# RWKV inverse: sending the products of half of the chunks to the other head's partitions

## The chip, the core and the metric

The kernel runs on one core of a Trainium2 chip. A core has a matrix engine (TensorE, in the profile PE for matmuls and PEld for weight loads), VectorE (DVE), ScalarE (ACT), GpSimd (POOL) and DMA queues that SyncE (SP) issues. TensorE reads both operands from SBUF and writes into PSUM, which has eight banks of 2 KB on each of 128 partitions; DVE and ACT carry results from PSUM back to SBUF. The metric is the device time of one execution in microseconds, the median of several runs. All arithmetic here is fp32.

## The reference

The program is a two-layer backbone over 1024 latent tokens and 256 context tokens. The change touches one branch of the first layer, a bidirectional RWKV-7 scan with 8 heads of width 64:

```python
def step(S, inp):
    r_t, k_t, v_t, w_t, a_t, kk_t = inp
    Skk = jnp.einsum('dbhvk,dbhk->dbhv', S, kk_t)
    S = S * w_t[..., None, :] - Skk[..., :, None] * (kk_t * a_t)[..., None, :] + v_t[..., :, None] * k_t[..., None, :]
    return S, jnp.einsum('dbhvk,dbhk->dbhv', S, r_t)
```

The kernel doesn't step token by token. It cuts the tokens into 20 chunks of 64 and writes each chunk as matrix products. Within a chunk the corrections by earlier tokens form a unit triangular 64x64 system; its inverse is needed once for each chunk, head and direction.

## The kernel before

**Streams and units.** A column tile `ct` holds two heads, head 0 on partitions 0 to 63 and head 1 on 64 to 127. Two streams (`rwkv_stream`) each work through two column tiles, and `lockstep` advances them in turn. Each column tile has ten units: a unit (`rwkv_unit`) takes two chunks of each direction, so NJ = 4 pieces `j` (0 and 1 forward, 2 and 3 backward) for each of two heads. That makes 2 streams x 2 column tiles x 10 = 40 units. `pace` runs unit q+1 beside the chain of unit q (`rwkv_chain`), which carries the state from chunk to chunk through the PSUM tiles `ch`.

**What a unit does.** Decays are scanned and exponentiated (lines 692 to 706, DVE and ACT), operands AR, KB and RZ are built (711 to 717, POOL and DVE), and `pa` takes the products of AR and KB (729), which DVE masks into MN (732). MT is one minus the triangular part (744), `pk` holds transposes of KB (750) that ACT copies to KT (752).

**The inverse (762 to 781).** The transposed inverse TT starts from blocks of width 2 and doubles the width five times, b = 2, 4, 8, 16, 32. A doubling has three groups of products, called turns here: *px* multiplies MT by Tm (769) and DVE masks it into Xs (771); *pz* multiplies TT by Xs (775) and ACT copies it to the next Tm (777); *pt* multiplies Xs by TT (779) and ACT copies it back to TT (780). Before the first doubling a turn *px0* multiplies MT by the identity (764). The last doubling has no pz. So a unit has 1 + 4 x 3 + 2 = 15 turns. Each turn is 8 products of 64x64 by 64x64 (4 pieces, 2 heads). `halves` sends head 0's from partitions 0 to 63 to PSUM partitions 0 to 63 and head 1's from 64 to 127 to 64 to 127: of the four 64x64 quarters of the array, the two on the diagonal are used. In the trace a turn is 16 records, since an fp32 product is two records of PE and of PEld.

**PSUM.** Each stream has two banks under the tag `rec`. Every tile of that tag took one bank or less before, so there were two buffers, used in turn. A new tile in a buffer waits for the readers of the one before it.

**Order.** In this stage the Tile framework's scheduler orders each engine's instructions when the program is built; each engine then runs its own list strictly in that order as far as waits go, so an instruction that waits holds up what is behind it. Up to 1178 us the stage shares TensorE with the output projection of layer 0 (tiles `oa`); from there to about 1925 us it is alone.

Of the kernel before, what the change touches and what calls it, by code (L numbers as in the profile page):

```python
# [149 lines left out]
class K:  # L150
# [494 lines left out]
    def rwkv_unit(s, st, ct, gi):  # L645

        nc, rp = s.nc, s.rp
        X = s.RX[ct]
        L = 64 * NG
        NJ = 2 * NG  # L650
# [3 lines left out]
        H = [slice(0, 64), slice(64, 128)]  # L654
# [4 lines left out]
        def flat(t):  # L659
            return t.rearrange("p a b -> p (a b)")  # L660

        def rec(*sh):
            return s.psum(f"rec{st}", (128, NJ) + sh)

        r, k, kk = tl("ur", [64]), tl("uk", [64]), tl("ukk", [64])
        par = s.tn[st] % 2
        s.tn[st] += 1
# [1 line left out]
        TT, RZ, MT = s.tt[st, par], s.rz[st, par], s.mt[st]  # L669
        SV = X["sv", gi] = tl("SV", [2, 2, 64], 2)  # L670
# [52 lines left out]
        yield  # L723
        MN = tl("MN", [2, 2, 64], 2)
        mP = s.m("mP").rearrange("p (j a b) -> p j a b", a=2, b=64)
        pa = [rec(2, 64) for h in range(2)]
        for j in range(NJ):
            for h in range(2):
                s.mm(pa[h][:, j].rearrange("p a b -> p (a b)"), kb(j, h),
# [5 lines left out]
        def dj(t):  # L735
            return t.rearrange("p (d j) b -> p d j b", d=2)

        def bj(name):
            m_ = s.m(name).rearrange("p (d b) -> p d b", d=2)
            return m_.unsqueeze(2).to_broadcast([128, 2, NG, m_.shape[2]])  # L740
# [3 lines left out]
            nc.vector.scalar_tensor_tensor(MT[H[h]], MN[H[h], :, 0, h], -1.0,  # L744
                                           ident[H[h], H[h]].unsqueeze(1).to_broadcast([64, NJ, 64]), ALU.mult, ALU.add)
        KT = tl("KT", [2, 64], 2)
        pk = [rec(64) for h in range(2)]
        for j in range(NJ):
            for h in range(2):
                s.tr(pk[h][:, j], kb(j, h), ident[H[h], H[h]])  # L750
# [3 lines left out]
        nc.vector.tensor_mul(dj(TT), dj(MT), bj("m1"))  # L754
        yield

        def halves(fn):
            for j in range(NJ):
                for h in range(2):
                    fn(j, H[h])  # L760

        Tm = tl("Tm", [64], 2)
        px = rec(64)
        halves(lambda j, Q: s.mm(px[Q, j], MT[Q, j], s.m("id2")[Q]))
        nc.vector.tensor_mul(dj(Tm), dj(px), bj("l1"))
        yield
        for b in (2, 4, 8, 16, 32):
            px = rec(64)
            halves(lambda j, Q: s.mm(px[Q, j], MT[Q, j], Tm[Q, j]))
            Xs = tl("Xs", [64])  # L770
            nc.vector.tensor_mul(dj(Xs), dj(px), bj(f"l{b}"))  # L771
            yield
            if b < 32:
                pz = rec(64)
                halves(lambda j, Q: s.mm(pz[Q, j], TT[Q, j], Xs[Q, j]))
                Tm = tl("Tm", [64], 2)
                nc.scalar.copy(Tm, pz)
            pt = rec(64)
            halves(lambda j, Q: s.mm(pt[Q, j], Xs[Q, j], TT[Q, j]))
            nc.scalar.copy(TT, pt)  # L780
            yield
        X["u", gi] = {"E2": E2, "MN": MN, "KT": KT, "SV": SV, "TT": TT, "RZ": RZ}

    def rwkv_chain(s, st, ct, gi):
        nc, rp = s.nc, s.rp
        X = s.RX[ct]
        H = [slice(0, 64), slice(64, 128)]
        U = X["u", gi]
        SV, TT, MN, KT, E2, RZ = (U[k] for k in ("SV", "TT", "MN", "KT", "E2", "RZ"))
# [16 lines left out]
        for n in range(NG):  # L806
# [8 lines left out]
            pu = ch()  # L815
            for d, j in enumerate(js):
                for h in range(2):
                    s.mm(pu[H[h], d], TT[H[h], j], w[H[h], d])
            nc.vector.tensor_copy(both(SV, n)[H[0], :, 1, 0], pu[H[0]])
            nc.scalar.copy(both(SV, n)[H[1], :, 1, 1], pu[H[1]])  # L820
            yield
# [1226 lines left out]
```

## Time and profile before

| | us |
|---|---|
| median of 3 runs (3821.68 to 3825.0) | 3823.33 |
| the profiled execution's own time | 3834.97 |
| span of the profile | 3833.2 |
| PE busy in the span | 3442.4 (90%) |
| DVE, ACT, POOL busy | 2197.4, 1510.3, 1118.5 |
| the RWKV stage in the span, about | 966 to 1925 |

A row of the windows view gives a stretch of the span, its length, the busy time of each engine with the number of instructions, then the granted TensorE clock as a share of full speed, the share of the DMA engines and GB/s. A row of the timeline gives start, length, engine, line, operation, output and inputs, shapes and the number of instructions merged. A PE record's length includes the time until its result is in PSUM, so neighbouring records overlap and "busy" is not "issuing at its peak". A row of the view by tile gives minimum, median and maximum duration in ns, first and last start in us.

### The profile page before, as it was taken

What the parts mean: (1) busy time and instruction counts of PE and PEld (TensorE: products, weight loads), DVE (VectorE), ACT (ScalarE), POOL (GpSimd) and SP (SyncE); (2) the same over time, 40 slices, a digit from 0 to 9 for tenths busy, and PEclk for the clock granted to TensorE, in tenths of its full rate; (3) what the DMA queues carried; (4) which work ended last, traced back from release to release, by engine and by line L of the source; (5) the groups of instructions that cost most, each with busy time, mean ns of one, the idle gap of its engine ahead of it and who ended that gap; (6) DMA issues with size and microseconds to landing.
All of it is one profiled execution on the core that took longest, in us unless ns stands there. A gap on an engine that the chain in (4) does not pass through costs nothing. (4 is left out here: it accounts for less than half of the span.)

```text
span 3833.2 us, 74118 instructions
## 1 busy us (share of the span) xinstructions
PE 3442.4 (90%) x29178; PEld 2751.3 (72%) x29178; DVE 2197.4 (57%) x4053; ACT 1510.3 (39%) x3219; POOL 1118.5 (29%) x1071
## 2 busy tenths in 40 slices
PE   7999998887898998899869999999999788999978
PEld 3687876664577776688747798788888666676757
DVE  3576587773456666555556804533344387777645
ACT  3232333333434546444433322322222225666751
POOL 0112267552323221212102112212122255444330
PEclk9999998997798989789969999999999898999989
DMA  6526454436443222211132332554554451000023
GB/s 235 178 75 198 135 183 148 161 117 183 139 124 98 69 65 70 75 48 44 26 110 102 110 97 90 184 183 128 162 160 153 135 164 58 23 22 21 20 79 112
DMA packets 394277, 429.57 MB, mean 112 GB/s; under 512 B 81377, under 2 KB 317761, under 8 KB 391369
## 3 DMA queue, kind: packets, MB, share of 16 engines
q1 hardware_dynamic: 393928, 424.83, 35.4%
q8 instruction: 230, 3.77, 0.4%
q14 instruction: 119, 0.97, 0.1%
HBM read 306.62 MB, written 118.05 MB: 111 GB/s over the span
## 5 line engine op out<-in xcount | busy, mean ns | idle before, releaser
L211 PE MATMUL mm<-hh,wh 128*128 128x512 f32 (+1 forms) x1640 | 634.8, 387 | 0.0
L211 PE MATMUL mm<-hh,wl 128*128 128x512 f32 (+1 forms) x1640 | 609.9, 372 | 1.0 <-POOL wl L358 1.0
L211 PE MATMUL mm<-hl,wh 128*128 128x512 f32 (+1 forms) x1640 | 608.6, 371 | 0.0
L358 POOL TENSOR_TENSOR wl<-wr,wh 128x1024 fp32r<-128x1024 f32 x99 | 249.0, 2519 | 538.8 <-ACT wh L357 482.8
L211 PEld LDWEIGHTS mm<-hh,wh 128*128 128x128 f32 x1640 | 314.4, 192 | 66.7 <-issue 12.7
L211 PEld LDWEIGHTS mm<-hl,wh 128*128 128x128 f32 x1640 | 314.2, 192 | 61.6 <-issue 10.6
L211 PEld LDWEIGHTS mm<-hh,wl 128*128 128x128 f32 x1640 | 313.3, 191 | 60.1 <-issue 3.4
L1793 POOL TENSOR_SCALAR aP<-aP,adn,one 128x1280 f32<-128x1280 f32 x128 | 192.6, 1504 | 283.2 <-DVE adn L1792 159.6
L211 PE MATMUL mm<-wh,hh 128*128 128x256 f32 x736 | 218.3, 297 | 0.0
L1786 DVE TENSOR_REDUCE amx<-sc 128x1 f32<-128x1024 f32 x128 | 156.0, 1219 | 102.6 <-PE sc L211 102.5
L211 PE MATMUL mm<-wl,hh 128*128 128x256 f32 x736 | 209.7, 285 | 2.4 <-POOL wl L358 1.6
L211 PE MATMUL mm<-wh,hl 128*128 128x256 f32 x736 | 209.6, 285 | 0.0
L214 PE MATMUL tp<-mk,aP 128*128 128x128 f32 x1280 | 183.2, 280 | 4.1 <-ACT aPT L1801 4.1
L1801 ACT COPY aPT<-tp 128x512 f32<-128x512 f32 x256 | 145.8, 588 | 84.2 <-PE tp L214 82.2
L211 PE MATMUL pv<-aPT,aV 128*64 128x256 f32 x1280 | 169.6, 396 | 0.3 <-DVE aG L1817 0.3
L214 PEld LDWEIGHTS tp<-mk,aP 128*128 128x128 f32 x1280 | 144.4, 142 | 35.4 <-issue 21.5
L357 ACT CAST wh<-wr 128x1024 fp32r<-128x1024 f32 x99 | 103.2, 1045 | 152.5 <-PE mm L211 120.8
L211 PE MATMUL sc<-akT,aqs 128*128 128x512 f32 x512 | 154.0, 423 | 1.4 <-DVE aqs L1771 1.1
L1074 POOL TENSOR_SCALAR sel<-mk,mdfd,mdt 128x128 f32<-128x128 f32 x160 | 128.4, 819 | 76.3 <-DVE E L1098 45.8
L771 DVE TENSOR_TENSOR Xs<-rec,mk 128x256 f32<-128x256 f32 x200 | 84.3, 423 | 110.5 <-PE rec L211 107.1
L211 PE MATMUL oa<-wh,yh 128*128 128x512 f32 x288 | 127.9, 444 | 21.2 <-DVE o L1225 10.4
L211 PEld LDWEIGHTS mm<-wl,hh 128*128 128x128 f32 x736 | 141.8, 193 | 3.2 <-POOL wl L358 2.0
(422 smaller groups left out, 8039.7 us busy)
## 6 DMA issues: line engine op xcount, KB each, us to landing
wr<-in_wcd SPq DMA_DIRECT2D x60, 512.0 KB, 5.4
adaw<-in_ada SPq DMA_DIRECT2D x48, 512.0 KB, 5.4
R<-rowd SPq DMA_DIRECT2D x20, 1024.0 KB, 5.5
wr<-in_wab SPq DMA_DIRECT2D x38, 512.0 KB, 4.0
yr<-y SPq DMA_DIRECT2D x36, 512.0 KB, 4.0
xt<-xtok SPq DMA_DIRECT2D x20, 512.0 KB, 5.2
SV<-vtd SPq DMA_DIRECT2D x320, 32.0 KB, 2.2
lva<-lv SPq DMA_DIRECT2D x19, 514.0 KB, 4.6
```

Of the source, the lines that this page charges most:

```text
L211: return s.nc.tensor.matmul(out, lhsT, rhs, start=start, stop=stop)
L214: return s.nc.tensor.transpose(out, in_, ident)
L357: nc.scalar.copy(hi, raw)
L358: nc.gpsimd.tensor_sub(lo, raw, hi.bitcast(F32))
L771: nc.vector.tensor_mul(dj(Xs), dj(px), bj(f"l{b}"))
L1074: nc.gpsimd.tensor_scalar(sel[:, h], s.m("slt"), s.dfd[:, o:o + 1], dtb[:, h:h + 1], ALU.mult, ALU.add)
L1786: nc.vector.tensor_reduce(mx[:, 1:2], ps, AX.X, ALU.max)
L1793: nc.gpsimd.tensor_scalar(P, P, dn[:, 3:4], s.one, ALU.mult, ALU.mult)
L1801: copy(out, pp.rearrange("p (a b) q -> p a (b q)", a=out.shape[1]))
```

## The change

For half of the pieces the products go to the other head's PSUM partitions. `turn` takes the place of `halves`: it gets for both operands the place of each (j, h), a partition half and an index, and a set `to` of pieces whose result goes to the other half than their head's. It sorts the products by quarter of the array (input half, output half) and issues one of each quarter in turn: (0,0), (1,1), (0,1), (1,0). `side` names the pieces that are moved: from the pt of the first doubling on, every turn has two products in each of the four quarters, so 12 of the 15 turns; px0, px and pz of the first doubling stay on the diagonal. What was moved once is multiplied where it lies, and the last turn brings everything back to its own head's half; only the index of a piece within TT then differs, which `rwkv_chain` looks up in `iTT`.

A `rec` tile is now always two banks, `(128, 2, 512)`. The bank of a product is the half of the partitions that its inputs are on, so that two quarters that write the same partitions write different banks. With two banks to a stream there is one buffer instead of two. From the second doubling on pz and pt share one tile, pz in the first 128 columns of both banks, pt in the next 128, and the copy of pz to Tm is issued behind the turn pt. The masks and copies read 128 columns of each of two banks instead of 256 columns of one.

```diff
-        pa = [rec(2, 64) for h in range(2)]
+        pa = s.psum(f"rec{st}", (128, 2, 512))
+        pa = [pa[:, h].rearrange("p (j a b) -> p j a b", j=NJ, a=2) for h in range(2)]
...
-        pk = [rec(64) for h in range(2)]
+        pk = s.psum(f"rec{st}", (128, 2, 512))
+        pk = [pk[:, h, :64 * NJ].rearrange("p (j b) -> p j b", j=NJ) for h in range(2)]
...
-        def halves(fn):
+        def turn(A, ia, B, ib, to, out, slot=None):
+            place, quad = {}, {}
             for j in range(NJ):
                 for h in range(2):
-                    fn(j, H[h])
+                    (c0, i), (c1, k) = ia[j, h], ib[j, h]
...
+                    c = 1 - h if j in to else h
+                    place[j, h] = c, 2 * c0 + slot(j) if slot else j
...
+                    quad.setdefault((c0, c), []).append((i, k, place[j, h][1]))
...
+            for n in range(NJ):
+                for q in ((0, 0), (1, 1), (0, 1), (1, 0)):
+                    for i, k, o in quad.get(q, [])[n:n + 1]:
+                        s.mm(out[H[q[1]], o // 2, 64 * (o % 2):64 * (o % 2) + 64], A[H[q[0]], i],
+                             s.m("id2")[H[q[0]]] if B is None else B[H[q[0]], k])
+            return place
...
-        for b in (2, 4, 8, 16, 32):
-            px = rec(64)
-            halves(lambda j, Q: s.mm(px[Q, j], MT[Q, j], Tm[Q, j]))
+        side = ((), (1, 3), (0, 3), (1, 3), (0, 3), ())
+        for n, b in enumerate((2, 4, 8, 16, 32)):
+            px = pt_()
+            iX = turn(MT, own, Tm, iT, side[n], area(px, 0), (lambda j: j // 2) if n else None)
             Xs = tl("Xs", [64])
-            nc.vector.tensor_mul(dj(Xs), dj(px), bj(f"l{b}"))
+            mask(Xs, area(px, 0), f"l{b}", n > 0)
             yield
+            pz = pt_()
             if b < 32:
-                pz = rec(64)
-                halves(lambda j, Q: s.mm(pz[Q, j], TT[Q, j], Xs[Q, j]))
+                iT = turn(TT, iTT, Xs, iX, (), area(pz, 0), (lambda j: j // 2) if n else None)
+            if n == 0:
                 Tm = tl("Tm", [64], 2)
-                nc.scalar.copy(Tm, pz)
-            pt = rec(64)
-            halves(lambda j, Q: s.mm(pt[Q, j], Xs[Q, j], TT[Q, j]))
-            nc.scalar.copy(TT, pt)
+                nc.scalar.copy(Tm.rearrange("p (b s) l -> p b (s l)", b=2), area(pz, 0))
+                pt = pt_()
+            else:
+                pt = pz
+            iTT = turn(Xs, iX, TT, iTT, side[n + 1], area(pt, 1), (lambda j: j % 2) if 0 < n < 4 else (lambda j: j // 2))
+            if n and b < 32:
+                Tm = tl("Tm", [64], 2)
+                nc.scalar.copy(Tm.rearrange("p (b s) l -> p b (s l)", b=2), area(pz, 0))
+            nc.scalar.copy(TT.rearrange("p (b s) l -> p b (s l)", b=2), area(pt, 1))
             yield
...
-                    s.mm(pu[H[h], d], TT[H[h], j], w[H[h], d])
+                    s.mm(pu[H[h], d], TT[H[h], iTT[j, h][1]], w[H[h], d])
```

The scheduler's order changes with it. Three places are shown. In the rows, rec0 and MT0 belong to stream 0, rec1 and MT1 to stream 1; a number behind x counts products, and the bracket names the engines whose results an instruction waits for.

First, TensorE in the middle of a unit, where both streams are doubling: px of stream 1, then pz and pt of stream 0, then pz and pt of stream 1. Before:

```order
L211 MATMUL rec1_3357_18654<-Tm_3352_18621,MT1_6812 64x64 [waits DVE_49]
L211 MATMUL rec1_3357_18654<-Tm_3352_18621,MT1_6812 64x64 x7
L211 MATMUL rec0_3359_18665<-Xs_3356_18652,TT00_6791 64x64 [waits DVE_49,Activation_49]
L211 MATMUL rec0_3359_18665<-Xs_3356_18652,TT00_6791 64x64 x7
L211 MATMUL rec0_3361_18676<-TT00_6791,Xs_3356_18652 64x64 [waits PE_49]
L211 MATMUL rec0_3361_18676<-TT00_6791,Xs_3356_18652 64x64 x7
L211 MATMUL rec1_3363_18693<-Xs_3358_18663,TT11_6807 64x64 [waits DVE_49]
L211 MATMUL rec1_3363_18693<-Xs_3358_18663,TT11_6807 64x64 x7
L211 MATMUL rec1_3365_18704<-TT11_6807,Xs_3358_18663 64x64 [waits PE_49]
L211 MATMUL rec1_3365_18704<-TT11_6807,Xs_3358_18663 64x64 x7
```

The same place of the changed program, with the px of stream 0 that follows:

```order
L211 MATMUL rec1_3208_18574<-Tm_3203_18541,MT1_6812 64x64 [waits Activation_49]
L211 MATMUL rec1_3208_18574<-Tm_3203_18541,MT1_6812 64x64 x7
L211 MATMUL rec0_3210_18585<-Xs_3207_18572,TT00_6791 64x64 [waits DVE_49]
L211 MATMUL rec0_3210_18585<-Xs_3207_18572,TT00_6791 64x64 x7
L211 MATMUL rec0_3210_18585<-TT00_6791,Xs_3207_18572 64x64 x8
L211 MATMUL rec1_3213_18616<-Xs_3209_18583,TT11_6807 64x64 [waits DVE_49]
L211 MATMUL rec1_3213_18616<-Xs_3209_18583,TT11_6807 64x64 x7
L211 MATMUL rec1_3213_18616<-TT11_6807,Xs_3209_18583 64x64 x8
L211 MATMUL rec0_3217_18643<-Tm_3211_18602,MT0_6801 64x64 [waits PE_49,Activation_49]
L211 MATMUL rec0_3217_18643<-Tm_3211_18602,MT0_6801 64x64 x7
```

The order of the turns is the same; pt has no wait of its own any more, since it writes pz's tile.

Second, ScalarE's copies at that place, stream 0 and then stream 1. Before:

```order
L777 COPY Tm_3360_18674<-rec0_3359_18665 128x256 [waits PE_49]
L780 COPY TT00_6791<-rec0_3361_18676 128x256 [waits PE_49,Activation_49]
L777 COPY Tm_3364_18702<-rec1_3363_18693 128x256 [waits PE_49]
L780 COPY TT11_6807<-rec1_3365_18704 128x256 [waits PE_49]
L842 COPY y_2936_16167<-ch1_3366_18714 128x2x64 [waits PE_49]
```

And in the changed program:

```order
L816 COPY Tm_3211_18602<-rec0_3210_18585 128x256 [waits PE_49]
L817 COPY TT00_6791<-rec0_3210_18585 128x256
L816 COPY Tm_3214_18633<-rec1_3213_18616 128x256 [waits PE_49]
L817 COPY TT11_6807<-rec1_3213_18616 128x256 [waits Activation_49]
L817 COPY TT00_6791<-rec0_3221_18665 128x256 [waits PE_49,Activation_49]
```

Before, the copies to Tm and TT waited for a turn each; now both read one tile and both come behind pt, with Tm first.

Third, TensorE at the start of a unit of stream 1: the transposes pk (L214) and px0, which reads the identity in mk2. Before (pk of head 1, the chain's products and stream 0's turns between them):

```order
L214 MATMUL rec1_3346_18579<-mk_60,KB_3333_18505 128x64 [waits DVE_49]
L214 MATMUL rec1_3346_18579<-mk_60,KB_3333_18505 128x64 x3
L211 MATMUL ch0_3362_18686<-w_3351_18619,TT01_6796 64x64 x2
L211 MATMUL rec0_3347_18593<-Xs_3343_18573,TT00_6791 64x64 [waits DVE_49,Activation_49]
L211 MATMUL rec0_3347_18593<-Xs_3343_18573,TT00_6791 64x64 x7
L211 MATMUL rec0_3349_18604<-TT00_6791,Xs_3343_18573 64x64 [waits PE_49]
L211 MATMUL rec0_3349_18604<-TT00_6791,Xs_3343_18573 64x64 x7
L211 MATMUL rec1_3353_18622<-mk2_6776,MT1_6812 64x64 [waits DVE_49,Activation_49]
```

And in the changed program:

```order
L214 MATMUL rec1_3187_18420<-mk_60,KB_3176_18348 128x64 [waits DVE_49,PE_49]
L214 MATMUL rec1_3187_18420<-mk_60,KB_3176_18348 128x64 x7
L211 MATMUL rec0_3188_18434<-Xs_3185_18415,TT00_6791 64x64 [waits DVE_49]
L211 MATMUL rec0_3188_18434<-Xs_3185_18415,TT00_6791 64x64 x7
L211 MATMUL rec0_3188_18434<-TT00_6791,Xs_3185_18415 64x64 x8
L211 MATMUL rec1_3193_18462<-mk2_6776,MT1_6812 64x64 [waits DVE_49,PE_49,Activation_49]
```

The transposes of both heads now stand together behind the second mask of MN, and px0 waits for the copies of both heads to KT, since all share the one buffer.

More of the change, by code (lines that the diff above doesn't have):

```diff
@@ L660, in flat @@
             return t.rearrange("p a b -> p (a b)")
-        def rec(*sh):
-            return s.psum(f"rec{st}", (128, NJ) + sh)
         r, k, kk = tl("ur", [64]), tl("uk", [64]), tl("ukk", [64])
@@ L755, in rwkv_unit @@
         yield
-        def halves(fn):
+        def turn(A, ia, B, ib, to, out, slot=None):
+            place, quad = {}, {}
             for j in range(NJ):
                 for h in range(2):
-                    fn(j, H[h])
+                    (c0, i), (c1, k) = ia[j, h], ib[j, h]
+                    assert c0 == c1
+                    c = 1 - h if j in to else h
+                    place[j, h] = c, 2 * c0 + slot(j) if slot else j
+                    assert slot or c == c0
+                    quad.setdefault((c0, c), []).append((i, k, place[j, h][1]))
+            assert len(set(place.values())) == 2 * NJ
+            for n in range(NJ):
[4 more added lines that the diff above has]
+            return place
@@ new lines, in half, with mask, area, pt_ @@
+        def half(t):
+            return t.rearrange("p (b s) l -> p b s l", b=2)
+        def mask(t, out, name, banked):
+            m_ = s.m(name).rearrange("p (d b) -> p d b", d=2)
+            m_ = m_.unsqueeze(1).to_broadcast([128, 2, 2, 64]) if banked else m_.unsqueeze(2).to_broadcast([128, 2, 2, 64])
+            nc.vector.tensor_mul(half(t), out.rearrange("p b (s l) -> p b s l", s=2), m_)
+        def area(t, i):
+            return t[:, :, 128 * i:128 * i + 128]
+        def pt_():
+            return s.psum(f"rec{st}", (128, 2, 512))
@@ L762, in rwkv_unit @@
         Tm = tl("Tm", [64], 2)
-        px = rec(64)
-        halves(lambda j, Q: s.mm(px[Q, j], MT[Q, j], s.m("id2")[Q]))
-        nc.vector.tensor_mul(dj(Tm), dj(px), bj("l1"))
+        own = {(j, h): (h, j) for j in range(NJ) for h in range(2)}
+        px = pt_()
+        iT, iTT = turn(MT, own, None, own, (), area(px, 0)), own
+        mask(Tm, area(px, 0), "l1", False)
         yield
-        for b in (2, 4, 8, 16, 32):
-            px = rec(64)
-            halves(lambda j, Q: s.mm(px[Q, j], MT[Q, j], Tm[Q, j]))
+        side = ((), (1, 3), (0, 3), (1, 3), (0, 3), ())
@@ L770, in rwkv_unit @@
+        for n, b in enumerate((2, 4, 8, 16, 32)):
+            px = pt_()
+            iX = turn(MT, own, Tm, iT, side[n], area(px, 0), (lambda j: j // 2) if n else None)
             Xs = tl("Xs", [64])
-            nc.vector.tensor_mul(dj(Xs), dj(px), bj(f"l{b}"))
+            mask(Xs, area(px, 0), f"l{b}", n > 0)
             yield
+            pz = pt_()
             if b < 32:
-                pz = rec(64)
-                halves(lambda j, Q: s.mm(pz[Q, j], TT[Q, j], Xs[Q, j]))
+                iT = turn(TT, iTT, Xs, iX, (), area(pz, 0), (lambda j: j // 2) if n else None)
+            if n == 0:
@@ L781, in rwkv_unit @@
+            nc.scalar.copy(TT.rearrange("p (b s) l -> p b (s l)", b=2), area(pt, 1))
             yield
-        X["u", gi] = {"E2": E2, "MN": MN, "KT": KT, "SV": SV, "TT": TT, "RZ": RZ}
+        X["u", gi] = {"E2": E2, "MN": MN, "KT": KT, "SV": SV, "TT": (TT, iTT), "RZ": RZ}
     def rwkv_chain(s, st, ct, gi):
@@ L788, in rwkv_chain @@
         U = X["u", gi]
-        SV, TT, MN, KT, E2, RZ = (U[k] for k in ("SV", "TT", "MN", "KT", "E2", "RZ"))
+        SV, (TT, iTT), MN, KT, E2, RZ = (U[k] for k in ("SV", "TT", "MN", "KT", "E2", "RZ"))
         if gi == 0:
```

## The prediction

> **What bounds the kernel now.** I read the windows view first, because the change acts in one stage only. Its rows give the stretch, its length, PE, PEld, DVE, ACT and POOL busy, then clock, DMA share and GB/s; the rows of DVE alone are of the mask MN, two for each unit.
>
> ```profile
> 966.00:1178.00 212.00, 191.32 (x2083) 142.84 (x2084) 112.57 (x189) 83.89 (x189) 67.33 (x65) 0.86 0.43 130
> 1178.00:1925.00 747.00, 668.32 (x12960) 560.87 (x12960) 444.10 (x1013) 367.12 (x1025) 162.61 (x203) 0.89 0.22 59
> 1500.00:1600.00 100.00, 76.44 (x1079) 59.39 (x1080) 61.42 (x126) 52.98 (x122) 26.23 (x32) 0.76 0.29 85
> 1632.00:1895.00 263.00, 245.43 (x5150) 211.89 (x5147) 147.54 (x364) 117.85 (x364) 51.79 (x66) 0.94 0.15 39
> 1178.00:1925.00 747.00, 45.24 (x70) 0.89 0.22 59
> 1632.00:1895.00 263.00, 18.01 (x28) 0.94 0.15 39
> ```
>
> From 1178 us on the stage stands alone: 747 us with 35 of the 40 units. PE is busy 93% of the calm stretch 1632 to 1895, DVE 56%, ACT 45%. There 14 units, so 7 periods of one unit of each stream, take 263 us: **37.6 us a period**. "Busy" counts drains, so I ask the view of groups for that stretch what the remaining idle time waits for, and the timeline whether TensorE issues without a pause.
>
> ```profile
> L211 PE MATMUL rec<-AR,KB 64*128 64x128 f32 x224 | 22.3, 308 | 14.3 <-POOL AR L713 13.9 <-DVE KB L715 0.3
> ```
>
> ```profile
> 1719.89 1.11 PE L211 MATMUL rec<-Tm,MT 64*64 64x64 f32 x16
> ...
> 1723.41 1.15 PE L211 MATMUL rec<-Tm,MT 64*64 64x64 f32 x32
> 1724.48 0.33 PE L211 MATMUL ch<-SV,mk 128*64 128x64 f32 x2
> 1724.74 0.68 PE L211 MATMUL rec<-Xs,TT 64*64 64x64 f32 x16
> 1725.26 0.63 PE L211 MATMUL rec<-TT,Xs 64*64 64x64 f32 x16
> ...
> 1726.43 0.68 PE L211 MATMUL rec<-Xs,TT 64*64 64x64 f32 x16
> 1726.94 0.63 PE L211 MATMUL rec<-TT,Xs 64*64 64x64 f32 x16
> 1727.51 0.45 PE L211 MATMUL ch<-SV,MN 128*64 128x64 f32 x8
> 1727.89 1.15 PE L211 MATMUL rec<-Tm,MT 64*64 64x64 f32 x32
> ```
>
> Of the 17.6 us that PE is idle (263 less 245.43), 13.9 are one wait, AR for POOL at the start of a unit. From 1723.41 to 1727.89, a *joint step* (both streams do one doubling), one group follows the other without a hole: px of both (x32), pz and pt of one stream, products of the chain, pz and pt of the other, chain. So in joint steps TensorE's issue is what ends last, and a turn that issues faster shortens the step.
>
> **What a turn costs, and what four quarters make of it.** The second turn in an x32 row adds 1.15 - 0.68 = 0.47 us, and it is 8 pairs of records (one of each diagonal quarter), so a pair takes 0.059 us. With four quarters used, four records share such a slot: 4 slots instead of 8, **0.235 us less for each of 12 turns**. For 40 units that is 480 x 0.235 = 113 us, or 127 at the mean clock of 0.89: the most that can be gained.
>
> Four at once is not in the trace. Two halves of it are:
>
> ```profile
> 1729.84 0.27 PE L211 MATMUL ch<-SV,MN 128*64 128x64 f32 x1
> 1729.85 0.27 PE L211 MATMUL ch<-SV,RZ 128*64 128x64 f32 x1
> 1729.94 0.22 PE L211 MATMUL ch<-SV,MN 128*64 128x64 f32 x1
> 1729.95 0.22 PE L211 MATMUL ch<-SV,RZ 128*64 128x64 f32 x1
> ...
> 1737.07 1.16 PE L211 MATMUL rec<-AR,KB 64*128 64x128 f32 x14
> ```
>
> Chain products on the two column halves, which share all rows, start 0.01 us apart, and the second product's first record starts ahead of the first product's second: a free tile doesn't wait for a busy one. AR,KB uses two row halves, which share all columns and write two banks: 14 records of 128 columns would take at least 14 x 0.118 = 1.65 us one by one (twice the slot each), and took 1.16, so they run in pairs. The bounds are therefore 0 and 0.235 us a turn; I take 0.235, as each sharing that four quarters need stands in one of these rows.
>
> The Trainium skill, TensorE: Matmul & The Clock Gate, Part 3: Packing small matmuls, says that a weight load overlaps matmuls in flight only where the row group differs. Quarters (0,0) and (0,1) share a row group, so by that rule a turn would stay at 0.47, which is the slower rival below; the rows of 1729.84 disagree, since both products load all rows.
>
> **The terms, for one period.** Durations of the other engines come from the view by tile, a lone step (only one stream left doubling) from the timeline.
>
> ```profile
> L771 DVE TENSOR_TENSOR Xs<-rec,mk x200: 405/425/426, 983.7 to 1910.4; 128x256 f32<-128x256 f32 x100
> L777 ACT COPY Tm<-rec x160: 354/372/387, 985.8 to 1909.2; 128x256 f32<-128x256 f32 x160
> L732 DVE TENSOR_TENSOR MN<-rec,mk x80: 654/682/694, 969.6 to 1889.9; 128x512 f32<-128x512 f32 x80
> ```
>
> ```profile
> 1731.66 0.63 PE L211 MATMUL rec<-Tm,MT 64*64 64x64 f32 x16
> ...
> 1733.00 0.68 PE L211 MATMUL rec<-Xs,TT 64*64 64x64 f32 x16
> 1733.51 0.63 PE L211 MATMUL rec<-TT,Xs 64*64 64x64 f32 x16
> ...
> 1734.57 0.68 PE L211 MATMUL rec<-Tm,MT 64*64 64x64 f32 x16
> ```
>
> ```profile
> 1733.72 0.37 ACT L777 COPY Tm<-rec 128x256 f32<-128x256 f32 x1 [1.27 <-PE rec L211]
> 1734.25 0.37 ACT L780 COPY TT<-rec 128x256 f32<-128x256 f32 x1
> ```
>
> *The new chain of one stream.* A turn's result is read 0.05 us after its end (pz ends 1733.68, Tm starts 1733.72). With one buffer, px waits for the copy to TT as well, and Tm is copied behind pt. One doubling is then px 0.45 (0.68 less 0.235), mask 0.425, pz and pt 0.23 + 0.45, Tm 0.37, TT 0.37, and four handovers of 0.05: **2.5 us**.
>
> *Joint steps.* Six turns shrink by 1.41: 4.48 becomes 3.07. That stays above one stream's 2.5, above two masks (0.85) and above four copies (1.49) with the chain's few. For restarts of 0.05 (0.68 against 0.63) and worse packing I give back 0.2: -1.2 each. From 1719.89, when the second stream joins, to 1731.66, when the first is done, there are three in a period: **-3.6**.
>
> *Lone steps.* 1731.66 to 1734.57 is 2.91 us. The chain gives 2.5, with chain products in the gaps 2.6: -0.3, twice a period: **-0.6**. Here the waits for pt and the copy to TT, 0.23 + 0.37, eat most of what the turns save.
>
> *First steps of the earlier stream.* Between these two px, of one stream, the other sets up its unit:
>
> ```profile
> 1711.33 1.12 PE L211 MATMUL rec<-Tm,MT 64*64 64x64 f32 x16
> ...
> 1718.29 1.06 PE L211 MATMUL rec<-Tm,MT 64*64 64x64 f32 x16
> ```
>
> A doubling takes 7 us there, at half clock (a turn of 1.06 instead of 0.63) and behind setup. Four turns with four quarters save 0.94 to 1.9; most goes into the same wait for POOL, so between 0 and 1.9 I take **-0.5**.
>
> *Setup.* All transposes now wait for the second MN mask, 0.68 later than the first, and px0 for the copies of both heads to KT: 0 to about 1.1 us. Behind pk stand the other stream's turns, which cover a part: **+0.5**. In the first doubling pt waits for Tm's copy and the next px for TT's: 0 to 0.9 (turn 0.45, copy 0.37, handovers); this falls into the stalled stretch, so **+0.3**.
>
> *Masks and copies on two banks.* From L771 and L732 256 more elements cost 0.257, so the fixed part is 0.17: a second piece could cost nothing or up to 0.17. The element count is the same, so I take 0; the other end adds 0.5 to each doubling's chain. Less than nothing is excluded, as no element is saved.
>
> *Clock.* TensorE will pause more. 24 turns a period lose 5.6 of 35.1 us busy, so busy falls from 93% to 29.4 of 33.7, 87%; rows at 90% and 76% had clocks of 0.86 and 0.76, though with long DMA gaps. **+0.5**, bounds 0 and 3.
>
> Sum: -3.6 - 0.6 - 0.5 + 0.5 + 0.3 + 0.5 = **-3.4 us a period**. 35 units are 17.5 periods: -60. In the five units ahead of 1178 TensorE is shared with the output projection and DMA is at 0.43; half of it, 2.5 x 1.7: -4. Together **-64 us**: 3835 of the profiled execution becomes 3771, and from the median of 3823.3, which lies 0.3% lower, **3759**.
>
> **Rivals.** *Only two quarters run at a time* (the change doesn't do what it says). Turns stay at 0.47, the waits remain. Joint steps don't care: TensorE's 4.48 covers the chain, which is then 3.2 us (px 0.68, mask 0.425, pz and pt 0.47 + 0.68, copies 0.74, handovers 0.2). Two lone steps cost +0.3 each, setup and first doubling +0.8: +1.4 a period, +24 us, **3847, slower**. It decides if a turn gets less than some 0.06 us shorter, since 24 turns must pay 1.4. For it: no row shows three tiles at work. Against: the overtaking rows above.
>
> *The clock follows the busy share.* At 0.84 instead of 0.94 a period of 33.7, of which I take 80% as TensorE-bound, gets 3.2 longer: net -0.7, -12 us, **3811**. For: the row of 1500 to 1600. Against: the low clock there goes with long holes, while joint steps stay dense.
>
> *Evacuation takes over.* If each mask and copy costs 0.17 more, each of five doublings takes 0.5 longer, 2.5 a period: -0.9 is left, -16 us, **3807**. For: ACT already follows each turn. Against: ACT is busy 45% only. The Trainium skill, TensorEngine Tiling (Array Packing), PSUM Bottleneck, says that after such a speedup the copies out of PSUM may become the bottleneck; the 2.5 us chain, nearly half of it copies and a mask, leans that way, and the joint 3.07 does not.
>
> **How the numbers follow.** Forecast 62% at 3759, its own range 3705 to 3795 (-6.5 to -1.5 a period); two quarters 14%; clock 11%; evacuation 13%. 3705 to 3830 leaves out most of the slower case and the deepest gains, about two tenths. A measurement tells some 0.2%, 8 us, from no change. Slower: the first rival and tails of the last two, 17%; within: 8%; faster: 75%.
>
> **What would show it.** A four-quarter turn of 16 records should read about 0.40 to 0.45 us instead of 0.63 to 0.68, in an unbroken pair of turns 0.23 apart; if it reads 0.63, the first rival holds. px of both streams should recur every 3.1 us in joint steps and every 2.6 in lone ones; the row of MN should give 14 units in some 239 us. A clock below 0.88 in the calm stretch speaks for the second rival, DVE masks near 0.6 us or ACT copies near 0.54 for the third. The forecast falls if joint steps are rarer than three a period, or if the new order puts a waiting AR,KB ahead of turns that were ready.

## The result, and the profile after

| | us | ratio to before (95%) |
|---|---|---|
| forecast | 3759, range 3705 to 3830 | |
| before, median of 4 runs beside the changed kernel | 3822.98 | |
| changed, median of 4 runs (3788.40 to 3804.39) | 3795.82 | 0.9929 (0.9907 to 0.9951) |
| profiled execution, before and changed | 3834.97 and 3797.94 | |

The kernel is 27 us faster, 0.7%, where 64 us were forecast. The direction and the range held, the size did not: less than half came. The execution traced before lay 12 us above its median, the one of the changed kernel 2, so the traces differ by 37 us, some 10 more than the medians.

First the rows that answer to those of before. The windows view of the changed kernel (columns as before; the second piece is the row of the mask MN, DVE busy only):

```profile
966.00:1178.00 212.00, 181.74 (x2074) 131.73 (x2076) 117.01 (x192) 81.04 (x187) 70.39 (x67) 0.86 0.44 131
1178.00:1894.00 716.00, 601.67 (x12972) 473.79 (x12970) 446.45 (x1013) 354.20 (x1029) 158.63 (x203) 0.83 0.23 63
1500.00:1600.00 100.00, 71.32 (x1060) 51.84 (x1060) 50.77 (x102) 43.48 (x107) 21.09 (x27) 0.62 0.25 72
1624.00:1858.00 234.00, 18.04 (x28) 0.95 0.18 45
```

The stage ends 31 us earlier, and the calm stretch did better than forecast: the same 28 masks, 14 units, take 234 us instead of 263; the forecast was 239. What is new is the clock of the whole stage, 0.83 instead of 0.89, and 0.62 instead of 0.76 in the stretch around 1550.

The view by tile (minimum, median, maximum in ns) and the timeline of TensorE in joint steps of the changed kernel:

```profile
L783 DVE TENSOR_TENSOR Xs<-rec,mk x200: 361/425/426, 980.8 to 1881.2; 128x256 f32<-128x256 f32 x100
L816 ACT COPY Tm<-rec x120: 353/373/393, 990.0 to 1877.8; 128x256 f32<-128x256 f32 x120
L730 DVE TENSOR_TENSOR MN<-rec,mk x80: 627/681/693, 971.6 to 1853.0; 128x512 f32<-128x512 f32 x80
```

```profile
1706.82 0.46 PE L211 MATMUL rec<-Tm,MT 64*64 64x64 f32 x16 [0.22 <-ACT TT L817]
1707.10 0.41 PE L211 MATMUL rec<-Xs,TT 64*64 64x64 f32 x16
1707.33 0.41 PE L211 MATMUL rec<-TT,Xs 64*64 64x64 f32 x16
1708.32 0.46 PE L211 MATMUL rec<-Xs,TT 64*64 64x64 f32 x16 [0.57 <-DVE Xs L783]
...
1709.78 0.46 PE L211 MATMUL rec<-Tm,MT 64*64 64x64 f32 x16
```

A turn takes 0.41 to 0.46 us instead of 0.63 to 0.68, and of an unbroken pair the second starts 0.23 behind the first (1707.10 and 1707.33): four quarters do run at once. Masks and copies on two banks cost what they did (0.425, 0.373 and 0.681 against 0.425, 0.372 and 0.682). But where TensorE issued without a pause before, two rows now have a wait in brackets: for the copy to TT, and for the mask Xs.

Equal places of the program are better than equal times. These rows go from the first MN mask of unit 6 of the stage's order to that of unit 20 (beside the features of the second column tiles), to that of unit 26 (the change of column tiles), to that of unit 38, counting both streams' units as they come, from 0: 14, 6 and 12 units. Before, changed, and the first experiment, which has the changed kernel's buffer but only two quarters:

```profile
1187.30:1473.80 286.50, 262.51 (x5156) 220.44 (x5156) 179.67 (x412) 147.72 (x411) 66.86 (x84) 0.90 0.25 68
1473.80:1637.20 163.40, 135.48 (x2288) 108.72 (x2286) 101.05 (x210) 85.95 (x217) 37.94 (x47) 0.82 0.26 74
1637.20:1862.90 225.70, 211.03 (x4370) 181.91 (x4372) 125.61 (x314) 101.47 (x313) 46.49 (x60) 0.93 0.17 42
```

```profile
1187.60:1464.20 276.60, 243.04 (x5176) 192.34 (x5178) 179.39 (x412) 142.12 (x412) 65.03 (x84) 0.83 0.26 71
1464.20:1629.40 165.20, 124.56 (x2268) 93.69 (x2268) 100.72 (x210) 83.53 (x216) 37.33 (x47) 0.74 0.25 72
1629.40:1828.60 199.20, 179.78 (x4395) 144.42 (x4398) 127.71 (x314) 95.75 (x315) 45.08 (x60) 0.94 0.19 49
```

```profile
1191.30:1493.80 302.50, 274.84 (x5174) 226.79 (x5176) 180.94 (x412) 143.68 (x413) 65.64 (x84) 0.87 0.24 65
1493.80:1665.30 171.50, 138.28 (x2280) 110.49 (x2280) 99.43 (x211) 82.50 (x214) 37.48 (x47) 0.78 0.25 69
1665.30:1884.10 218.80, 206.16 (x4384) 174.25 (x4381) 127.51 (x313) 96.49 (x315) 45.18 (x60) 0.97 0.17 44
```

Beside the features the changed kernel gained 9.9 us in 7 periods, at the column change it lost 1.8 in 3, in the calm stretch it gained 26.5 in 6. At 3.4 a period these would have been 24, 10 and 20. So the calm stretch, from which the forecast was read, kept its promise, and the other two stretches did not. The diagonal kernel shows that such a stretch can't be read alone: in the calm one it is faster than the kernel before (218.8 us against 225.7), and slower in both others.

### The profile page after: what moved, and what is told of

Same layout as the page of the kernel before. It is cut to its first block, busy times and chain, and to the rows that moved or that the text cites. A ratio compares the mean times of both kernels' runs of the same rounds, so it can differ in the third digit from the quotient of the medians.

```text
span 3796.1 us, 74040 instructions
## 1 busy us (share of the span) xinstructions
PE 3366.2 (89%) x29178; PEld 2650.6 (70%) x29178; DVE 2208.6 (58%) x4053; ACT 1493.0 (39%) x3219; POOL 1116.6 (29%) x1071
## 5 line engine op out<-in xcount | busy, mean ns | idle before, releaser
L214 PE MATMUL tp<-mk,aP 128*128 128x128 f32 x1280 | 181.0, 278 | 5.0 <-ACT aPT L1838 5.0
L214 PEld LDWEIGHTS tp<-mk,aP 128*128 128x128 f32 x1280 | 142.5, 141 | 35.9 <-issue 20.4
```

Source lines behind the costliest of these rows:

```text
L214: return s.nc.tensor.transpose(out, in_, ident)
```

## The experiments

Ratios are to the kernel before on the same chip (3829 to 3837 us there), with 95% intervals.

### Quarters and buffer apart

The changed kernel with `side` empty keeps to the diagonal, with the buffer, the waits and the late copy to Tm of the change:

```diff
-        side = ((), (1, 3), (0, 3), (1, 3), (0, 3), ())
+        side = ((),) * 6
```

(places within a tile then follow the piece number in every turn, and masks are laid out for that.)

> The changed kernel, but no piece is sent to the other half: every turn keeps to the two quarters on the diagonal; the one buffer of two banks, the tile shared by pz and pt, and the late copy to Tm stay. It prices the buffer and the new waits alone. By the working on record this is the first rival: +1.4 us a period, 3847 us, and the calm stretch at some 39 us a period instead of 37.6. If the waits are what ate the missing 37 us of the forecast, they must cost more than that: the four quarters are worth some 60 to 110 us as in the calm stretch (4.4 us a period and more), so this kernel would read 3860 to 3900. If the missing gain lies elsewhere (the column change, the clock), it reads 3830 to 3850.

Measured: 3861.3, **1.0087** (1.0069 to 1.0104). The buffer and its waits cost 33 us, and the four quarters give back 1.0087 - 0.9929 = 1.58%, 60 us. That lies at the lower edge of the 3860 to 3900 that were expected if the waits ate the gain. By the prediction's own working the first rival put the waits at 24 us, and the quarters at 64 + 24 = 88. So of the 37 us that are missing some 9 lie with the waits and some 28 with the quarters, each with an error of some 10.

Next, the features of the second column tile begin earlier, in both kernels:

```diff
-            if gi == 4 and ct != cts[-1]:
+            if gi == 1 and ct != cts[-1]:
```

> The changed kernel, with the features of the second column tile begun beside unit 1 instead of unit 4. Theory A (the column change): the changed kernel finished its units of the first column tile 10 us earlier, but then waited for the features of the second, whose first unit began at 1543 us as before; with the features begun earlier that wait goes, and the time falls by 8 to 20 us to some 3776 to 3788. Theory B (the clock takes the gain back beside the features): the features cost the same wherever they lie, so the time stays within 6 us of 3796.

> The kernel before, with the same earlier features: the control of the run above. Theory A: before the change the inverse was slow enough to let the features finish nearly in time, so little is to be had: 3815 to 3825. If it gains as much as the changed kernel does (8 to 20 us), the column change cost both kernels alike and isn't where the forecast lost its gain.

Measured: changed 3786.14, **0.9886** (0.9866 to 0.9906); before 3803.7, **0.9929** (0.9915 to 0.9944). Theory A falls: the kernel before gains even more, so the column change cost both alike. As a pair they differ by 17.6 us.

Then the same pair with no features of the second column tiles at all: the ten groups are left out, and the second tiles read the data of the first.

```diff
-                side.append(s.alone(s.rwkv_prep(st, cts[cts.index(ct) + 1])))
+                s.RX[cts[1]] = {}
+                for x in (s.kk_d, s.vt_d, s.bv_d):
+                    x[cts[1]] = x[cts[0]]
```

> The kernel before, without the features of the second column tiles: their ten groups of projections are left out, and the second column tiles read the key directions, values and bonus terms of the first (that part of the computation is wrong). So no unit runs beside features, and the column change waits for none. It is one half of a pair with the next run. Units beside features should then cost about as much as those after the column change, 37 us a period: from the first MN mask of unit 12 to that of unit 52 some 365 us instead of 450, so a total of some 3740 to 3775.

> The changed kernel, with the same part left out. Theory E (the gain is lost beside the features: there TensorE's holes and the half clock take back what the four quarters save, and the column change waits for the features, not for the inverse): without features every period gains what the periods after the column change gained, 4.4 us, so the pair differs by 55 to 80 us, or 1.5 to 2.1%. Rival (the four quarters save less than thought everywhere, and the large gain after the column change was chance of one execution's clock): the pair differs by 18 to 40 us, as the two whole kernels do.

Measured: before 3738.53, **0.9773** (0.9750 to 0.9795); changed 3715.52, **0.9716** (0.9692 to 0.9740). (Where these expectations say unit 12 or 52, they count masks, two to a unit: units 6 and 26 here.) Theory E falls too: the pair differs by 23 us, not 55 to 80. From the first mask of unit 26 to that of unit 38 the kernel before now takes 209.4 us, where it took 225.7, though nothing of that stretch was edited, and the changed one 198.6, as it did:

```profile
1559.50:1768.90 209.40, 193.81 (x4363) 168.74 (x4360) 125.16 (x314) 100.45 (x312) 48.56 (x61) 0.94 0.18 46
```

```profile
1550.20:1748.80 198.60, 174.89 (x4358) 146.17 (x4358) 125.07 (x314) 96.38 (x312) 49.26 (x60) 0.90 0.19 49
```

With the features begun early the kernel before takes 209.7 us there as well:

```profile
1632.60:1842.30 209.70, 194.11 (x4390) 169.06 (x4392) 125.65 (x313) 100.78 (x313) 47.52 (x60) 0.95 0.18 45
```

TensorE's list is indeed another in that stretch. In the kernel before, the earlier stream's px stands ahead of the later stream's transposes, which come in two pieces; without second features (second fence), and with the features early too, the transposes stand together ahead of that px:

```profile
1750.72 0.68 PE L211 MATMUL rec<-Tm,MT 64*64 64x64 f32 x16
1751.79 0.46 PE L214 MATMUL rec<-mk,KB 64*128 64x64 f32 x4
1752.92 0.46 PE L214 MATMUL rec<-mk,KB 64*128 64x64 f32 x4
```

```profile
1630.86 0.70 PE L214 MATMUL rec<-mk,KB 64*128 64x64 f32 x8
...
1631.49 1.11 PE L211 MATMUL rec<-Tm,MT 64*64 64x64 f32 x16
```

So the 37 us a period on which the forecast stands belong to one order of the list; in two others the same kernel runs at 35. Of the 26.5 us gained there some 16 go with the order; in the two other orders the change gains 11 us (209.4 to 198.6) and 15 (209.7 to 195.0).

The diagonal kernel in these two surroundings:

> The changed kernel on the diagonal alone (all turns in two quarters, but one buffer and its waits), without the features of the second column tiles (that part of the computation is wrong). It stands between the pair that differed by 23 us, 3738.5 and 3715.5. Theory F (two parts with opposite signs in any order: the waits cost some 30 us, the quarters give back 50 to 60): 3762 to 3780. Rival (in the regular order without features the waits hide, and the quarters are worth little): 3738 to 3752.

> The changed kernel on the diagonal alone, with the features of the second column tile begun beside unit 1. It stands between the kernel before with that edit, 3803.7, and the changed kernel with it, 3786.1. Theory F: 3826 to 3850. Rival: 3800 to 3818.

Measured: 3775.93, **0.9844** (0.9829 to 0.9859), and 3841.91, **1.0015** (1.0000 to 1.0030). With them the split is there three times, each number a difference of ratios times 3830 (by the intervals, some 10 us either way):

| | buffer and waits | four quarters | net |
|---|---|---|---|
| as it is | +33 | -60 | -27 |
| features early | +33 | -49 | -16 |
| no second features | +27 | -49 | -22 |

That the change nets some 20 us, out of +30 and -50 to -60, is thus shown in three orders of the list. The traces, one execution each, say the same of the stage alone: from the first MN to the last product of a chain the buffer costs 26, 34 and 38 us, and the quarters give back 59, 53 and 53.

### Where in a period

Without second features several steps repeat from period to period to 0.01 us, so places can be compared. The table has means over the last four periods of the calm stretch, from the starts of the first records of the turns (px0, px) and of MN; "later" is the stream that joins last. Us:

| stretch of a period | before | changed | before, no 2nd features | diagonal, no 2nd | changed, no 2nd |
|---|---|---|---|---|---|
| three joint steps | 11.34 | 9.35 | 12.29 | 12.58 | 9.99 |
| last px but one of the later to MN of the earlier | 6.40 | 5.04 | 5.90 | 6.29 | 5.58 |
| of it, to the last px (a lone step) | 2.91 | 3.08 | 2.49 | 3.67 | 3.40 |
| MN to the first doubling | 4.80 | 5.84 | 5.83 | 5.82 | 5.82 |
| first doubling of the earlier to that of the later | 14.42 | 12.43 | 11.08 | 12.76 | 12.64 |
| period | 36.97 | 32.65 | 35.09 | 37.46 | 34.02 |

The last three columns tell buffer from quarters by place. Of the 2.4 us a period that the buffer costs there, 1.7 lie between the two first doublings; of the 3.4 that the quarters give back, 2.6 lie in the joint steps.

The lone step, timeline of the pair without second features, before and then changed:

```profile
1611.51 0.68 PE L211 MATMUL rec<-Tm,MT 64*64 64x64 f32 x16
...
1612.84 0.68 PE L211 MATMUL rec<-Xs,TT 64*64 64x64 f32 x16
...
1613.36 0.63 PE L211 MATMUL rec<-TT,Xs 64*64 64x64 f32 x16
1613.57 0.37 ACT L777 COPY Tm<-rec 128x256 f32<-128x256 f32 x1 [1.49 <-PE rec L211]
1614.00 0.68 PE L211 MATMUL rec<-Tm,MT 64*64 64x64 f32 x16
1614.09 0.37 ACT L780 COPY TT<-rec 128x256 f32<-128x256 f32 x1
```

```profile
1597.56 0.46 PE L211 MATMUL rec<-Tm,MT 64*64 64x64 f32 x16
...
1599.15 0.46 PE L211 MATMUL rec<-Xs,TT 64*64 64x64 f32 x16
1599.43 0.41 PE L211 MATMUL rec<-TT,Xs 64*64 64x64 f32 x16
...
1599.91 0.37 ACT L816 COPY Tm<-rec 128x256 f32<-128x256 f32 x1 [1.07 <-PE rec L211]
...
1600.18 0.38 ACT L817 COPY TT<-rec 128x256 f32<-128x256 f32 x1
...
1600.62 0.48 PE L211 MATMUL rec<-AR,KB 64*128 64x128 f32 x2
...
1601.03 0.46 PE L211 MATMUL rec<-Tm,MT 64*64 64x64 f32 x16
```

From pz to the next px it took 1.16 us before: Tm was copied beside pt, and px started ahead of the copy to TT. Now it takes 1.88, though the turns are shorter: pt ends at 1599.84, Tm and TT are copied behind it, and behind the copy to TT one product of AR,KB, whose turn it is in the list, delays px by 0.41 more.

The first doubling of the earlier stream, the same pair, before and then changed:

```profile
1662.17 1.21 PE L211 MATMUL rec<-AR,KB 64*128 64x128 f32 x16 [1.93 <-DVE SV L819]
...
1663.31 1.12 PE L211 MATMUL rec<-Xs,TT 64*64 64x64 f32 x16
...
1664.22 1.06 PE L211 MATMUL rec<-TT,Xs 64*64 64x64 f32 x16
...
1666.46 0.72 PE L211 MATMUL rec<-Tm,MT 64*64 64x64 f32 x16
```

```profile
1644.31 0.79 PE L211 MATMUL rec<-AR,KB 64*128 64x128 f32 x2 [1.93 <-DVE SV L856]
...
1645.44 2.07 PE L211 MATMUL rec<-AR,KB 64*128 64x128 f32 x14
...
1647.44 1.12 PE L211 MATMUL rec<-Xs,TT 64*64 64x64 f32 x16
...
1648.61 0.37 ACT L809 COPY Tm<-rec 128x256 f32<-128x256 f32 x1 [3.95 <-PE rec L211]
...
1649.54 0.71 PE L211 MATMUL rec<-TT,Xs 64*64 64x64 f32 x16
...
1650.80 0.71 PE L211 MATMUL rec<-Tm,MT 64*64 64x64 f32 x16
```

Both wait 1.93 us in the setup. Before, AR,KB then still ran at nearly full clock (0.95 granted; 16 records in 1.21 us), and pz came 1.14 us after its start; in the changed kernel the clock was at 0.50 already (14 records in 2.07), AR,KB stands in two pieces with chain products between, and pz came 3.13 us after it. The wait of pt for Tm (2.10 from pz to pt instead of 0.91) was paid back at the next px (1.26 instead of 2.24).

### Single waits

AR,KB of a unit given first place in the scheduler's order, so that they stand together, in both kernels:

```diff
+        with s.tc.high_priority():
             for j in range(NJ):
                 for h in range(2):
                     s.mm(pa[h][:, j]...
```

> The changed kernel, with the eight products AR,KB of a unit given first place in the scheduler's order, so that they stand together: 59 groups for 40 units as before the change, instead of 104. Theory C (scattered AR,KB): in the changed kernel single products of AR,KB stand ahead of turns that were ready, and the turn behind one started 0.42 us later; up to the next start AR,KB took 30.2 us from 1188 to 1464 and 26.4 us from 1629 to 1829, against 21.7 and 17.1 before. Together they fall back to 22 and 18, and the time falls by 12 to 24 us. Rival (filled gaps): the single products used time that nothing else could use, and together they only wait for POOL with the turns behind them: within 6 us, or slower. By the 0.9929 of the changed kernel to the one before: theory 0.987 to 0.990, rival 0.992 to 0.997.

> The kernel before with the same first place for AR,KB: 42 groups instead of 59. Control. They stood nearly together already, so theory C says within 8 us of the kernel before; a gain of over 12 us would say that first place is worth something by itself, not by undoing what the change scattered.

Measured: changed 3807.44, **0.9935** (0.9917 to 0.9952); before 3847.64, **1.0043** (1.0028 to 1.0058). Theory C falls as the cause of the total. The scattered products do delay turns, but in the traces the changed kernel takes 703 us from unit 6 to the end of the stage with AR,KB together, and 705 without. What first place costs, it costs earlier: from the first MN to that of unit 6, beside the output projection, 230 us instead of 216, and 227 instead of 218 in the kernel before.

Tm copied on VectorE, so that the two copies run side by side:

```diff
-                nc.scalar.copy(Tm...
+                nc.vector.tensor_copy(Tm...
```

> The changed kernel, with the copy of pz to Tm on VectorE instead of ScalarE (from the second doubling on), so that Tm and TT are copied side by side: the next px of the stream waits for one copy of 0.37 us instead of two that start 0.27 apart. Theory D (the chain of one stream, px, mask, pz, pt, copies, sets a joint step now): a step falls by about 0.27, four in a unit, two streams partly beside each other: 8 to 18 us less in all. Rival (TensorE's own issue or the setup sets the step): within 6 us; VectorE's masks queue behind the copies and give back what is gained.

> The kernel before, with the copy of pz to Tm on VectorE in every doubling. Control of the same edit in the changed kernel, which gained some 0.65%. Theory D (only in the changed kernel do the two copies behind pt stand one after the other ahead of px; before, pz's copy ran beside the turn pt): within 8 us of the kernel before. Rival (ScalarE is overloaded in both): 12 to 25 us faster.

> The changed kernel without the second features, with Tm copied on VectorE. With the whole kernel this edit gained 24 us, with three other edits it lost 17. Theory D (the two copies behind pt set the lone step): the step from the last px but one to the last of the later stream falls from 3.4 to 3.1 us, and the run from 3715 to 3690 to 3706. Rival (the gain came from another order of the list, not from the copy): 3710 to 3735.

Measured: changed 3780.6, **0.9864** (0.9833 to 0.9895); before 3837.79, **1.0023** (1.0009 to 1.0038); without second features 3719.45, **0.9702** (0.9685 to 0.9720) against 0.9716. A gain of 0.65% in one order and none in the other: the copies behind pt are not, by themselves, what the buffer costs.

Both KT copies ahead of the copies of AR into MN:

```diff
         for h in range(2):
             nc.scalar.copy(KT[:, :, h], pk[h])
+        for h in range(2):
             nc.scalar.copy(MN[H[h], :, 0, h], AR[H[h], :, 0])
```

> The changed kernel without the second features, with both copies to KT ahead of the two copies of AR into MN. Setup waits: from the MN mask to px0 of the earlier stream it takes 4.33 us, against 3.69 in the kernel before, since px0 waits for the second KT copy, which stands behind a copy of AR of 0.40. Theory: that stretch falls to 3.7 to 4.0, and the run by 5 to 11 us, to 3704 to 3711. Rival (px0 stands behind the products mm of the other stream anyway): 3712 to 3725.

> The whole changed kernel with both KT copies ahead of the copies of AR. Without second features this edit gained 0.5%: px0 came 0.44 us sooner, and the half clock that follows the setup's hole left most periods (13.7 us at half clock from unit 52 to 76 instead of 40.4). If the setup and the clock carry part of the waits in the whole kernel too: 0.987 to 0.990 of the kernel before, that is 10 to 22 us less than the changed kernel. Rival (the clock there was one execution's luck, or beside features other holes keep it low): 0.992 to 0.995.

Measured: without second features 3708.85, **0.9669** (0.9652 to 0.9686) against 0.9716; in the whole kernel 3807.77, **0.9923** (0.9895 to 0.9951) against 0.9929, nothing. Where it helped, px0 of the earlier stream came 3.89 us behind MN instead of 4.33, as expected, but its next px came no sooner (5.82 us in both). The gain shows one step later, and the clock came back with it, 0.96 where the same stretch had 0.90 above:

```profile
1539.60:1731.00 191.40, 169.85 (x4401) 139.30 (x4400) 125.42 (x313) 95.89 (x312) 47.77 (x60) 0.96 0.20 50
```

The first doubling of the earlier stream takes 7.96 us from its px to the next, where it took 9.53 (means of four periods); over the six periods that covers the 7.2 us between 198.6 and 191.4. Whether the earlier px0 brought the clock back, or the clock alone shortened the step, these runs don't separate.

Extra products in TensorE's holes, to hold the clock up:

```diff
+        if s.tn[st] > 4:
+            wm = s.psum("oa").rearrange("p (a b) -> p a b", a=8)
+            for _ in range(4):
+                s.mm(wm[:, :4], s.m("bd1"), KB[:, :, 1])
```

> The changed kernel with four extra products of 128x256 ahead of AR,KB in each unit from the sixth of the program on, into the free bank oa, read by nobody: TensorE works where it waited for POOL. Theory B (clock): from 1187 to 1464 the granted clock was 0.83 and 99 us went at half clock, against 61 us before the change; filled holes bring the clock there to 0.90 or more and the total down by 5 to 15 us, though the fillers themselves take up to 1.7 us of issue a unit. Theory A: the clock rises too, but the column change still waits for the features, so the time stays or grows by up to 30 us for the fillers' own issue.

Measured: 3839.81, **1.0026** (1.0014 to 1.0037). Beside the features the clock rose from 0.83 to 0.92, and the stretch still took 282.8 us instead of 276.6, with some 34 us of busy time of the extra products in it; in the calm stretch, with fewer holes, it took 236.9 instead of 199.2. It tells the price of the clock from that of the extra work too poorly to settle anything.

### A better version

> The changed kernel with AR,KB together, the features of the second column tile begun beside unit 1, and both copies to KT ahead of the two copies of AR into MN, so that px0 waits for two ScalarE copies instead of three. If the three are independent: -16 for the features as measured above, -12 to -24 for AR,KB, -0.3 a unit or -5 to -10 for KT: 0.976 to 0.985 of the kernel before. If AR,KB only filled gaps: 0.985 to 0.990.

> The changed kernel with AR,KB together, features early, KT copies first, and Tm copied on VectorE: the best version if the edits add up. 0.9823 with the first three, and 0.0065 for Tm: 0.974 to 0.979 of the kernel before. If ScalarE's queue was relieved by the first three already: 0.979 to 0.984.

> The changed kernel with KT copies first and the features begun beside unit 1, without the regrouping of AR,KB, which by itself did nothing. If both edits hold and add up: 0.9886 less 0.003 to 0.005, so 0.983 to 0.986, as good as the version with all three (0.9823). If AR,KB in one piece matters once the setup is shorter, it stays at 0.986 to 0.990.

Measured: AR,KB together, features early and KT first 3764.48, **0.9823** (0.9804 to 0.9842), faster than both kernels; with Tm on VectorE besides 3773.08, 0.9868 (0.9845 to 0.9891); without AR,KB together 3788.28, 0.9872 (0.9846 to 0.9898). In the best one the calm stretch runs at full clock, 185.9 us against 199.2:

```profile
1611.70:1797.60 185.90, 165.04 (x4406) 134.39 (x4402) 127.37 (x313) 98.10 (x314) 44.11 (x59) 1.00 0.20 49
```

Its edits don't add up one by one: grouping AR,KB, worth nothing alone, is worth 0.5% here, and copying Tm on VectorE changes its sign. The kernel before was not run with all three edits; the early features alone bring it to 0.9929, so at most 1.1 of the 1.8% can be put down to the change together with the other two.

## Why the prediction was wrong in size

*Four quarters at once: right.* Turns shrank by the 0.23 us forecast, and the second of a pair starts 0.23 behind the first (1707.10 and 1707.33). The rule of the Trainium skill that the prediction weighed (TensorE: Matmul & The Clock Gate, Part 3: Packing small matmuls) would, by the prediction's working, have left it 0.47 behind; these rows disagree. The first rival is out, but its price for the waits, +24, was near what the diagonal kernels showed, +27 to +33.

*The step that failed: joint steps, "4.48 becomes 3.07 ... -1.2 each ... -3.6".* The length after was right, 9.35 / 3 = 3.12 us. The length before was not: 4.48 is the longest of three unlike steps, whose sum is 11.34 (the last has one turn fewer, the first overlaps the other stream's first doubling). Measured are -2.0 us a period in the whole kernels and -2.3 in the pair without second features. The rows quoted in the prediction had it: from 1719.89 to 1731.66 is 11.77 us, and 11.77 - 9.2 = 2.6. The turns were miscounted too. Between those rows 16 start, not 18, and two of them, px and pz of the later stream's first doubling, keep to two quarters, as this row of the changed kernel shows; 14 x 0.235 is 3.3 us, not 4.2.

```profile
1704.42 0.63 PE L211 MATMUL rec<-Xs,TT 64*64 64x64 f32 x16
```

Beside the features the steps gained about as much, 2.4 us a period counted from the first px of a pair (13.4 to 11.0, means of seven), 2.8 from the second. At 2.0 to 2.8 instead of 3.6 the term is 14 to 28 us too large over 17.5 periods. This is an estimate: at the column change the steps can't be lined up like this.

The calm stretch lost nothing against the forecast all the same; the gain is missing beside the features and at the column change. Beside the features the other part of it went between the first MN of the earlier stream and the joint steps, 17.3 us instead of 15.7 (means of six periods), where the forecast had +0.3 for setup, first steps and first doubling together.

*"35 units are 17.5 periods": failed.* The calm stretch gained 4.4 us a period, more than the -3.4 of the sum, but the surplus goes with the order that the list of before had there. The same kernel with its list disturbed elsewhere runs the stretch 16 us faster, and in the pair without second features the change gains 1.9 us a period beside units 6 to 19 (245.3 to 231.9 us) and 1.8 after unit 26. Beside the features it gained 1.4, at the column change nothing.

*Lone steps, -0.3: wrong in sign.* 3.08 instead of 2.91, and in the regular pair 3.40 instead of 2.49. The chain itself was near: in the whole kernel it takes 2.4 us (px at 1712.43 to the end of TT's copy at 1715.26, less 0.42 for one AR,KB product ahead of pz), in the regular pair 3.0, since pz there stands behind products of the state's chain. But the forecast let px wait for nothing besides it, while AR,KB products of the next unit now stand in front of it; the prediction named something like it, a waiting AR,KB ahead of ready turns, as a way to fall. That comes back in part at the next MN, since those products are then done: the whole stretch to MN is shorter by 0.3 to 1.4.

*First steps, -0.5, first doubling, +0.3, and clock, +0.5: together mis-sized.* The stretch is 2.0 shorter in the whole kernels and 1.6 longer in the regular pair, so it goes with the order. Where it is longer, the half clock that meets AR,KB and pz behind the setup's hole is seen in the rows. The clock rival's condition (below 0.88 in the calm stretch) didn't occur, 0.94; but beside the features the clock went from 0.90 to 0.83 and at the column change from 0.82 to 0.74. By the granted clock the three stretches hold some 147 us at half clock before and some 201 in the changed kernel, so the clock can have taken at most about 27 us, an estimate for a TensorE that sets the time throughout; the forecast's +0.5 a period makes 9. The lower clock goes with the shorter turns: without second features the diagonal kernel has 0.94, 0.92 and 0.92 in the three stretches, and with the same buffer and four quarters it is 0.91, 0.80 and 0.90. How many microseconds the clock really cost was not isolated.

*Setup, +0.5:* +1.0 in the whole kernels, 0 in the regular pair. *Masks and copies on two banks, 0:* right (0.425, 0.373 and 0.681 us, as before), and the evacuation rival is out. What the prediction cites for that rival is said there of a fourfold speedup; here it is twofold at most.

*The first five units, -4:* from the first MN to that of unit 6, at 1187 us, the two kernels differ by -1.8 (217.8 to 215.9 us).

What stays open: how the missing gain beside the features divides between joint steps, setup and clock, since the three overlap, and which single wait carries the +30 of the buffer. The lone step and the first doubling show it at their places in one regular order, but no single edit took it away in the whole kernel.

## What to carry to other kernels

When a loop has unlike steps, sum them; one step that is seen running without a hole may be the longest, as here, and not the typical one, and the gain of a faster engine is the sum of what each step has above its other chain. A saving read from one stretch may be a property of that stretch's instruction order: test it with a harmless edit elsewhere before multiplying it. A change that trades buffers for speed should be run once with the buffers alone; here that gave +30 and -50 to -60, which the total of -27 hides.

## What the runs showed of the hardware

- Four 64x64 quarters with fp32 products start their 16 records in 0.23 us, where the two diagonal ones took 0.47, in two row groups and two column groups, with two banks for the same partitions.
- A single product of AR,KB (64x128, two records) between turns holds the next turn back by 0.41 to 0.42 us at full clock, while 16 records of them in a row took 1.16 us.
- Shorter turns alone (four quarters instead of the diagonal, same buffer, no second features) brought the granted clock from 0.94, 0.92 and 0.92 to 0.91, 0.80 and 0.90 in the three stretches; in the best version the calm stretch has 1.00 with the same turns.
- Small edits that leave the turns as they are moved this kernel by 0.65% down (Tm on VectorE), 0.43% up (AR,KB together, before) and 0.45% up (Tm on VectorE, in the best version): about the size of the change itself. The changed kernel's own four runs spread over 16 us; those of before spread over 3.3 beside it, and over 17 on another chip, with 13 runs.
